# A two-layer encoder kernel on one core: operand sums of the feed-forward part in tiles of their own, split sooner, another order of units in the down projection, and one more weight group by Strassen's scheme

## The chip, the cores and the metric

The kernel runs on one core of a Trainium2 chip. The metric is the device time of one execution in microseconds (us). The time shown for a kernel is the median of its runs.

## The reference, cut to what matters

Two layers work on 512 tokens of width 1024. Each has a token mixer, cross attention into 256 memory tokens and an output projection, which this change leaves alone, and then the feed-forward part:

```
def conv_ffn(h, w_up, conv_w, conv_b, w_down):
    u = h @ w_up                       # 1024 -> 5632
    c = depthwise causal convolution of u over the tokens, width 3, + conv_b
    a, g = jnp.split(c, 2, axis=-1)    # 2816 each
    return (jax.nn.silu(g) * a) @ w_down
...
h = rms_norm(x, ffn_norm[i])
x = x + conv_ffn(h, w_up[i], conv_w[i], conv_b[i], w_down[i])
```

All of it is in fp32.

## The kernel before, in words

**Products.** An fp32 operand is split into a rounded high part and the low remainder (`parts_of`, L1277 to L1279 for activations: the cast on ScalarE at L1278, the subtraction on VectorE at L1279). A product is three matmuls, high by high, high by low and low by high (`product`, L407 to L409). Weights come by DMA into a `raw` tile and are split into `whi` and `wlo` (cast on ScalarE, subtraction on VectorE, L257 and L260).

**Strassen's scheme.** Where the text says "seven", a 2x2 block of products is formed from 7 products instead of 8, with 256 columns in the moving operand instead of 512. That needs sums of the operands. Sums of weights are made on GpSimd: `block_sums` issues four additions (L285) into a tile `wsum`, of which there are two, and `combined` splits the raw part (L308, L309) and the sums (L311, L312). `SEVEN` (L140) lists which groups of the up projection go this way: the halves "ua" 5, 6, 8 and 9 of both layers. `up_by_seven` (L1213 to L1244) forms them, with one copy on ScalarE (L1238) and six additions on VectorE (L1239 to L1244) behind the matmuls.

**The feed-forward part.** `ffn` works through 11 groups of 256 hidden columns in three parts of 4, 4 and 3 groups. For each group there is a block "ua" (the half a) and a block "ug" (the gate g) of the up projection, each with two halves n = 0, 1 of 128 columns. `conv` (L1248 on VectorE, L1250 on ScalarE, L1251 and L1252 on VectorE) follows each, then the gate's silu (L1446, ScalarE), the product with a (L1448, VectorE) into a tile `cvo`, and the split of that product into two tiles `mid`. Behind a part's last group comes the down projection of the part (`down`), in four blocks c of 256 output columns. In the last part of layer 0 all four blocks, and in the last part of layer 1 the block 3, use eight products and no sums; the others use seven. A unit (c, m) is the contribution of the part's group m to block c: seven steps of three matmuls. Three of the steps, `own`, need only the group's own `mid` tiles: steps 1 and 2 those of its half n = 0, step 0 that of n = 1. Four, `mixed`, need sums of the two halves: steps 5 and 4 the first two sums, steps 6 and 3 the other two.

**Sums of the activations.** `mid_sums` calls `combine` (L1281 to L1290), four subtractions of 128x256. For the last group of a part they run on VectorE into two `cvo` tiles, and their split follows at once. For the other groups they run on GpSimd into one `wsum` tile of 128x1024, from the same two buffers as the sums of weights, and their split is put off: `behind` places it after the third `conv` that follows (`convs[0] == 3`).

**What sets the order.** TensorE runs in the order of the program. For VectorE, ScalarE and GpSimd a list scheduler orders the instructions when the kernel is built. In `down` the units (0, 0) to (0, nq-2) and (1, 0) come first, then, to give the last group's sums time, `own` of (0, nq-1), `own` of (1, 1), `mixed` of (0, nq-1), `mixed` of (1, 1), and so on. When a block c is complete, `decode` (L1369 to L1377) adds its four PSUM banks into the residual stream. The banks are taken in rotation, so block 2 gets those of block 0.

```
own, mixed = steps[:3], steps[3:]
seq = [(0, m, steps) for m in range(nq - 1)] + [(1, 0, steps), (0, nq - 1, own), (1, 1, own), (0, nq - 1, mixed)]
seq += [(1, 1, mixed)] + [(1, m, steps) for m in range(2, nq)]
```

Of the kernel before, what the change touches and what calls it, by code (L numbers as in the profile page):

```python
# [11 lines left out]
F32 = mybir.dt.float32  # L12
# [9 lines left out]
S = 512  # L22
# [114 lines left out]
    return out  # L137


SEVEN = [("ua", l, q) for l in range(2) for q in (5, 6, 8, 9)]  # L140
SUMS_AT = {1:(4,5),2:(0,1),3:(2,3)}
TURNS = ('mm', 'mm', 'sm', 'sm', 'lg', 'lg', 'tp', 'tp')

# [41 lines left out]
def trunk(ctx, tc, head_d, x_t, mem_t, wpack, cols_a_d, cols_d, conv_d, gate_d, rel_bias, diff_lambda, consts, onehot, out):  # L185
    nc = tc.nc
    mm = nc.tensor.matmul
    V, A, G = nc.vector, nc.scalar, nc.gpsimd
# [65 lines left out]
    at = [0]  # L254
# [70 lines left out]
    def sum_tile():  # L325
        return sum_pool[0].tile([128, WTILE], F32, name="wsum", bufs=2)
# [172 lines left out]
    E = mybir.EngineType  # L499
    load = nc.sync.dma_start  # L500
    with tc.tile_pool(name="ini", bufs=1) as ip, tc.manual_schedule(engines={E.Activation, E.DVE, E.Pool, E.SP}):
# [34 lines left out]
        parts, acc, split_w = [], [None], [None]  # L536
# [631 lines left out]
    def ffn(pool, l, acc):  # L1168
# [37 lines left out]
            refill()  # L1206

        def ctile():
            return pool.tile([128, S], F32, name="cvo", bufs=6)

        def up(i, n):
            p, = take(1)
# [34 lines left out]
        def conv(p, j):  # L1247
            V.tensor_mul(p, p, rB)  # L1248
            c = ctile()
            first = A.activation(c, p, AF.Identity, scale=cv[l][:, 2, j:j + 1], bias=cv[l][:, 3, j:j + 1])  # L1250
            V.scalar_tensor_tensor(c[:, 1:], p[:, :S - 1], cv[l][:, 1, j:j + 1], c[:, 1:], op0=ALU.mult, op1=ALU.add)  # L1251
            final = V.scalar_tensor_tensor(c[:, 2:], p[:, :S - 2], cv[l][:, 0, j:j + 1], c[:, 2:], op0=ALU.mult, op1=ALU.add)  # L1252
            if later:
                convs[0] += 1
                if convs[0] == 3:
                    convs[0] = 0
                    behind(first, final)
            return c
# [19 lines left out]
            A.copy(hi, t)  # L1278
            V.tensor_sub(lo, t, hi.bitcast(F32))  # L1279

        def combine(b2, b1, bh, bl, fh, fl, E, parts):  # L1281
            t = [ctile(), ctile()] if E is V else [sum_tile()]
            q = [blk(i, 256) for i in range(4)]
            at = lambda i: t[i // 2][:, q[i % 2]] if E is V else t[0][:, q[i]]
            for i, x, y in ((0, b1[:, right], b1[:, left]), (1, b2[:, right], at(0)), (2, b2[:, right], b1[:, right]),
                            (3, b2[:, left], at(1))):
                ins = E.tensor_sub(at(i), x, y)  # L1287
                if E is G:
                    tc.keep_in_program_order(ins)
            parts(t)  # L1290
            return q
# [6 lines left out]
        def mid_sums(c2, ops, E):  # L1298
            h, lo = (pool.tile([128, 2 * S], F32R, name="mid2", bufs=8) for _ in range(2))

            def parts(t):
                for i, x in enumerate(t):
                    c = blk(i, 2 * S // len(t))
                    if E is V:
                        parts_of(x, h[:, c], lo[:, c])
                    else:
                        later.append((x, h[:, c], lo[:, c]))
            q = combine(*c2, *ops, E, parts)
            return operands([h[:, c] for c in q], [lo[:, c] for c in q], *ops)

        later, convs = [], [0]
# [8 lines left out]
        def scaled(k):  # L1320
            t = ctile()
            A.activation(t, xT[k], AF.Copy, scale=c_ffn(l, k))
            return t

        def token_sums(ks):
            (bh, bl), (fh, fl) = (tokens[k] for k in ks)
            tiles = [split_tiles(pool, "vs", 12) for _ in range(2)]

            def parts(t):
                for i, (hi, lo) in enumerate(tiles):  # L1330
                    parts_of(t[0][:, blk(i, S)], hi, lo)
            combine(scaled(ks[0]), scaled(ks[1]), None, None, None, None, G, parts)
            h, lo = ([t[i][:, c] for t in tiles for c in (left, right)] for i in range(2))
            sums_of[ks] = operands(h, lo, bh, bl, fh[:, left], fl[:, left])

        place = [(2, left), (0, left), (0, right), (1, left), (1, right), (2, right), (3, left)]
        steps, close = (1, 2, 0, 5, 4, 6, 3), {2: 0, 5: 2, 6: 3, 3: 1}

        def down(base, nq, mids, pairs, last, acc2):
            first = used[0]  # L1340
            whole = [plan[first + c][0][0] == "dw" for c in range(4)]
            banks, seen = {}, [set() for _ in range(4)]

            def start(c):
                begin(("dw" if whole[c] else "dn", l, base, c))
                banks[c] = take(2 if whole[c] else 4)

            def emitted(c, m):
                if m == nq - 1 or m % 2:
                    release(first + c, 1 if whole[c] else 2, m == nq - 1)  # L1350

            def seven(c, m, some=steps):
                while len(made) <= first + c or len(made[first + c]) <= m:
                    refill()
                for i in some:
                    b, h = place[i]
                    (hi, lo), (bh, bl) = made[first + c][m][i], mids[m][i]
                    for t, (w, v) in enumerate(((hi, bh), (hi, bl), (lo, bh))):
                        mm(banks[c][b][:, h], w, v, start=b not in seen[c], stop=m == nq - 1 and t == 2 and i in close)  # L1359
                        seen[c].add(b)  # L1360
                if some[-1] != steps[-1]:
                    return
                emitted(c, m)
                if m == nq - 1:
                    decode(c)

            def decode(c):
                b, x1, x2, u, y = banks[c], xT[2 * c], xT[2 * c + 1], ctile(), ctile()[:, left]
                A.copy(u[:, left], b[2][:, left])  # L1369
                V.tensor_add(x1, x1, b[0])  # L1370
                V.tensor_add(y, u[:, left], b[2][:, right])
                V.tensor_add(u[:, right], y, b[1][:, right])
                V.tensor_add(y, y, b[3][:, left])
                V.tensor_add(x2, x2, b[1])
                V.tensor_add(x1, x1, u)
                x2v = x2.rearrange("p (h c) -> p h c", h=2)
                V.tensor_add(x2v, x2v, y.unsqueeze(1).to_broadcast([128, 2, 256]))  # L1377
                if last and l == 1:
                    for n in (2 * c, 2 * c + 1):
                        nc.sync.dma_start(out[n], xT[n])  # L1380

            def eight(c, n, m0, m1, total=nq):
                parts = whole_piece(first + c)
                product(banks[c][n], parts, n, pairs, range(2 * m0, 2 * m1), 2 * total)

            if all(whole):
                for c0 in (0, 2):
                    cs = (c0, c0 + 1)
                    for c in cs:
                        start(c)  # L1390
                        for n in range(2):
                            eight(c, n, 0, nq - 1)
                        emitted(c, 1)
                    for c in cs:
                        for n in range(2):
                            eight(c, n, nq - 1, nq)
                            update(2 * c + n, banks[c][n], lambda k: c_attn(1, k), acc2)
                            nc.sync.dma_start(xres[2 * c + n], xT[2 * c + n])
                        emitted(c, nq - 1)
                return  # L1400
            own, mixed = steps[:3], steps[3:]
            seq = [(0, m, steps) for m in range(nq - 1)] + [(1, 0, steps), (0, nq - 1, own), (1, 1, own), (0, nq - 1, mixed)]
            seq += [(1, 1, mixed)] + [(1, m, steps) for m in range(2, nq)]
            seq += [(c, m, steps) for c in ((2,) if whole[3] else (2, 3)) for m in range(nq)]
            for c, m, some in seq:
                if c not in banks:
                    start(c)
                seven(c, m, some)
            if whole[3]:
                start(3)  # L1410
                eight(3, 0, 0, nq)
                V.tensor_add(xT[6], xT[6], banks[3][0])
                nc.sync.dma_start(out[6], xT[6])
                eight(3, 1, 0, nq - 1, nq - 1)
                V.tensor_add(xT[7], xT[7], banks[3][1])
                for t, p, queue in zip((left, right), take(2), (nc.sync, nc.scalar)):
                    p = p[:, :S // 2]
                    parts = made[first + 3]
                    product(p, parts[-2:], 1, [(bh[:, t], bl[:, t]) for bh, bl in pairs[-2:]])
                    V.tensor_add(xT[7][:, t], xT[7][:, t], p)  # L1420
                    queue.dma_start(out[7, :, t], xT[7][:, t])

        base, acc2 = 0, None
        for part, nq in enumerate(HALVES):
            mids, pairs = [], []
            last = part == len(HALVES) - 1
            for q in range(base, base + nq):
                c2, ops, at, cs = [], [], {}, {}
# [11 lines left out]
                for n in range(2):  # L1440
# [13 lines left out]
                    else:  # L1454
                        m = mid_tile()
# [104 lines left out]
```

## Time and profile before

| | |
|---|---|
| median of three runs | 1152.81 us (1152.59 to 1152.91) |
| profiled execution | 1153.93 us |
| its span | 1152.0 us |
| granted TensorE clock | 1.00 |
| TensorE busy | 1141.9 us, 99% |
| VectorE busy | 931.4 us, 81% |
| ScalarE busy | 616.4 us, 54% |
| GpSimd busy | 270.1 us, 23% |

Times in the views below count from the start of the span. In a timeline each row gives the start, the time from the start of the row's first to the end of its last instruction, the engine, line and operation, the tiles, and in brackets the idle time before it with what ended it. A matmul's own duration runs past the start of the next, since matmuls are pipelined; what counts is the distance between starts. TensorE's rows in the down projection are L1359.

### The profile page before, as it was taken

How to read it: one execution, taken by the hardware profiler on the slowest of the kernel's cores; microseconds unless marked ns; L12 is line 12 of the kernel's file. 1: busy time of each engine (PE TensorE's matmuls, PEld its weight loads, DVE VectorE, ACT ScalarE, POOL GpSimd, SP SyncE). 2: the span in 40 equal slices, each digit the busy share in tenths (PEclk: the TensorE clock that was granted, in tenths of full speed). 3: DMA queues.
4: the chain of work that ended last, by engine and by line, in shares of the span. 5: the costliest groups of instructions: out<-in, count | busy, mean ns of one | idle time of the engine just before them, and what ended most of it. 6: DMA issues, size and time to landing. Idle time of an engine off the chain costs nothing.

```text
span 1152.0 us, 17410 instructions
## 1 busy us (share of the span) xinstructions
PE 1141.9 (99%) x6527; PEld 993.4 (86%) x6527; DVE 931.4 (81%) x1531; ACT 616.4 (54%) x1080; POOL 270.1 (23%) x318
## 2 busy tenths in 40 slices
PE   9999999999999999999999999999999999999998
PEld 7888888888889888898888888988888989899888
DVE  7676778688889789999677637777898988999987
ACT  6676686556554454445457634535664434544552
POOL 0000000003364423740000000000245432476241
PEclk9999999999999999999999999999999999999999
DMA  8522242133314332344252220333232343224312
GB/s 286 175 82 87 78 142 74 57 109 92 110 56 146 93 92 73 93 128 126 71 176 73 94 97 16 92 126 126 73 92 74 95 126 104 89 76 137 105 51 101
DMA packets 39666, 117.86 MB, mean 102 GB/s; under 512 B 4768, under 2 KB 7257, under 8 KB 39583
## 3 DMA queue, kind: packets, MB, share of 16 engines
q1 hardware_dynamic: 39150, 116.37, 32.0%
q8 instruction: 51, 0.84, 0.3%
q10 hardware_dynamic: 432, 0.39, 0.1%
q14 instruction: 33, 0.26, 0.1%
HBM read 112.54 MB, written 4.21 MB: 101 GB/s over the span
## 4 chain that ended last, share of the span: by engine, by line
PE 80%; DVE 13%; ACT 4%; issue 2%; POOL 1%; ACTq 0%; POOLq 0%; DVEq 0%
PE ps_mm L385 6%; PE ps_mm L408 6%; PE ps_mm L407 6%; PE ps_mm L409 6%; PE ps_mm L387 6%; PE ps_mm L386 6%; PE ps_lg L1359 3%; PE ps_sm L408 3%; PE ps_sm L407 3%; PE ps_sm L409 3%; PE ps_mm L1359 3%; PE ps_tp L224 3%; PE ps_lg L1233 3%; PE ps_tp L1359 2%; PE ps_sm L1359 2%; DVE mid L1279 2%
## 5 line engine op out<-in xcount | busy, mean ns | idle before, releaser
L260 DVE TENSOR_TENSOR wlo<-raw,whi 128x1024 fp32r<-128x1024 f32 (+5 forms) x166 | 188.7, 1148 | 74.7 <-ACT whi L257 73.8
L257 ACT CAST whi<-raw 128x1024 fp32r<-128x1024 f32 (+5 forms) x166 | 157.9, 967 | 104.9 <-PE ps_mm L408 24.3
L385 PE MATMUL ps_mm<-whi,xsh 128*128 128x512 f32 (+2 forms) x328 | 126.3, 385 | 0.0
L387 PE MATMUL ps_mm<-whi,xsl 128*128 128x512 f32 (+2 forms) x328 | 123.0, 375 | 0.0
L386 PE MATMUL ps_mm<-wlo,xsh 128*128 128x512 f32 (+2 forms) x328 | 122.8, 374 | 0.0
L407 PE MATMUL ps_mm<-xsh,whi 128*128 128x512 f32 x310 | 121.8, 393 | 0.0
L408 PE MATMUL ps_mm<-xsl,whi 128*128 128x512 f32 x310 | 120.9, 390 | 0.0
L409 PE MATMUL ps_mm<-xsh,wlo 128*128 128x512 f32 x310 | 120.8, 390 | 0.0
L285 POOL TENSOR_TENSOR wsum<-raw 128x256 f32<-128x256 f32 (+1 forms) x108 | 87.8, 834 | 117.5 <-DMA raw<-in_wpack_dram 64.1
L1287 POOL TENSOR_TENSOR wsum<-cvo 128x256 f32<-128x256 f32 x40 | 33.9, 848 | 226.7 <-DVE cvo L1448 140.9
L407 PE MATMUL ps_sm<-xsh,whi 128*128 128x512 f32 x202 | 78.6, 389 | 0.0
L408 PE MATMUL ps_sm<-xsl,whi 128*128 128x512 f32 x202 | 78.6, 389 | 0.0
L409 PE MATMUL ps_sm<-xsh,wlo 128*128 128x512 f32 x202 | 78.6, 389 | 0.0
L312 DVE TENSOR_TENSOR wlo<-wsum,whi 128x1024 fp32r<-128x1024 f32 (+1 forms) x54 | 70.6, 1307 | 8.9 <-ACT whi L311 8.9
L311 ACT CAST whi<-wsum 128x1024 fp32r<-128x1024 f32 (+1 forms) x54 | 51.9, 962 | 39.8 <-POOL wsum L285 39.5
L385 PEld LDWEIGHTS ps_mm<-whi,xsh 128*128 128x128 f32 x328 | 61.7, 188 | 11.4 <-issue 1.0
L387 PEld LDWEIGHTS ps_mm<-whi,xsl 128*128 128x128 f32 x328 | 61.7, 188 | 11.3
L386 PEld LDWEIGHTS ps_mm<-wlo,xsh 128*128 128x128 f32 x328 | 61.8, 188 | 10.1
L409 PEld LDWEIGHTS ps_mm<-xsh,wlo 128*128 128x128 f32 x310 | 58.2, 188 | 12.1
L407 PEld LDWEIGHTS ps_mm<-xsh,whi 128*128 128x128 f32 x310 | 58.2, 188 | 11.9 <-issue 0.3
L408 PEld LDWEIGHTS ps_mm<-xsl,whi 128*128 128x128 f32 x310 | 58.3, 188 | 11.9 <-DVE xsl L366 0.4
L1263 POOL MEMSET xsh<- 128x128 f32 x2 | 0.4, 210 | 277.5 <-PE ps_sm L408 191.0
(428 smaller groups left out, 3144.9 us busy)
## 6 DMA issues: line engine op xcount, KB each, us to landing
raw<-in_wpack_dram SPq DMA_DIRECT2D x178, 512.0 KB, 3.6
xt<-in_x_t_dram SPq DMA_DIRECT2D x15, 256.0 KB, 5.2
raw<-in_wpack_dram SPq DMA_DIRECT2D x15, 256.0 KB, 2.8
raw<-in_wpack_dram SPq DMA_DIRECT2D x8, 384.0 KB, 3.3
xres<-xt SPq DMA_DIRECT2D x8, 256.0 KB, 3.4
xt<-xres SPq DMA_DIRECT2D x8, 256.0 KB, 5.7
out_dram<-xt SPq DMA_DIRECT2D x7, 256.0 KB, 2.0
bt<-bias_d SPq DMA_DIRECT2D x6, 256.0 KB, 4.3
```

The lines of the kernel that those rows point to most:

```text
L257: ins = A.copy(hi[:, c], raw[:, c])
L260: V.tensor_sub(lo[:, c], raw[:, c], hi[:, c].bitcast(F32))
L285: tc.keep_in_program_order(getattr(G, "tensor_" + op)(o, x, y))
L311: A.copy(h1[:, m], wsum[:, m])
L312: V.tensor_sub(l1[:, m], wsum[:, m], h1[:, m].bitcast(F32))
L385: mm(p, sh[k][:, blk(b)], hi, start=k == 0, stop=False)
L386: mm(p, sh[k][:, blk(b)], lo, start=False, stop=False)
L387: mm(p, sl[k][:, blk(b)], hi, start=False, stop=k == KT - 1)
L407: mm(p, hi[:, blk(n)], bh, start=i == first, stop=False)
L408: mm(p, hi[:, blk(n)], bl, start=False, stop=False)
L409: mm(p, lo[:, blk(n)], bh, start=False, stop=i == last)
L1359: mm(banks[c][b][:, h], w, v, start=b not in seen[c], stop=m == nq - 1 and t == 2 and i in close)
```

## The change

Five edits. `SEVEN` gains the gate half of group 9 in layer 0. The sums of activations that GpSimd makes go into two `cvo` tiles of their own instead of a `wsum` tile, so that their split is two of 128x512 instead of one of 128x1024; there are seven `cvo` buffers instead of six. Their split is placed after the second `conv` instead of the third. In `down`, for parts of four groups, unit (1, 1) comes whole ahead of the last group's unit (0, 3), which comes whole too; for the part of three groups the order stays. The scratch memory for descriptors of dynamic DMAs is halved.

```
-SEVEN = [("ua", l, q) for l in range(2) for q in (5, 6, 8, 9)]
+SEVEN = [("ua", l, q) for l in range(2) for q in (5, 6, 8, 9)] + [("ug", 0, 9)]
...
-            return pool.tile([128, S], F32, name="cvo", bufs=6)
+            return pool.tile([128, S], F32, name="cvo", bufs=7)
...
-                if convs[0] == 3:
+                if convs[0] == (2):
...
-        def combine(b2, b1, bh, bl, fh, fl, E, parts):
-            t = [ctile(), ctile()] if E is V else [sum_tile()]
+        def combine(b2, b1, E, t, parts):
...
-            q = combine(*c2, *ops, E, parts)
+            q = combine(*c2, E, [ctile(), ctile()], parts)
...
-            combine(scaled(ks[0]), scaled(ks[1]), None, None, None, None, G, parts)
+            combine(scaled(ks[0]), scaled(ks[1]), G, [sum_tile()], parts)
...
-            seq = [(0, m, steps) for m in range(nq - 1)] + [(1, 0, steps), (0, nq - 1, own), (1, 1, own), (0, nq - 1, mixed)]
-            seq += [(1, 1, mixed)] + [(1, m, steps) for m in range(2, nq)]
+            seq = [(0, m, steps) for m in range(nq - 1)] + [(1, 0, steps)]
+            if nq > 3:
+                seq += [(1, 1, steps), (0, nq - 1, steps)] + [(1, m, steps) for m in range(2, nq)]
+            else:
+                seq += [(0, nq - 1, own), (1, 1, own), (0, nq - 1, mixed), (1, 1, mixed), (1, 2, steps)]
...
-    nc = _bacc.Bacc("TRN2", target_bir_lowering=False, num_devices=1, dynamic_dma_scratch_size=512)
+    nc = _bacc.Bacc("TRN2", target_bir_lowering=False, num_devices=1, dynamic_dma_scratch_size=256)
```

Three places show how instructions move; the numbers in names are those of the buffers. The first is TensorE behind unit (1, 0) in the first part of layer 0, in the kernel before: `mid_3313` and `mid_3411` belong to the last group, `mid_2943` to group 1.

```order
L1359 MATMUL ps_mm_3426<-mid_3313,whi_3342 128x256
...
L1359 MATMUL ps_mm_3426<-mid_3313,whi_3344 128x256
...
L1359 MATMUL ps_sm_3428<-mid_3411,whi_3342 128x256 x2
...
L1359 MATMUL ps_lg_3508<-mid_2943,whi_3382 128x256
...
L1359 MATMUL ps_lg_3508<-mid_2943,whi_3384 128x256
...
L1359 MATMUL ps_tp_3510<-mid_3040,whi_3382 128x256 x2
...
L1359 MATMUL ps_sm_3428<-mid2_3414,whi_3344 128x256
```

And in the changed kernel, where `mid_2948` and `mid_3043` belong to group 1 and `mid_3324` and `mid_3420` to the last group.

```order
L1358 MATMUL ps_lg_3517<-mid_2948,whi_3393 128x256
...
L1358 MATMUL ps_tp_3519<-mid_3043,whi_3393 128x256 x2
...
L1358 MATMUL ps_tp_3519<-mid2_3063,whi_3395 128x256
...
L1358 MATMUL ps_lg_3518<-mid2_3063,whi_3393 128x256
...
L1358 MATMUL ps_mm_3435<-mid_3324,whi_3353 128x256
...
L1358 MATMUL ps_sm_3437<-mid_3420,whi_3353 128x256 x2
```

Where the last group's first step stood, group 1's unit (1, 1) now stands, with all its seven steps; the last group's first step, its step 0 and its first mixed step come behind it. The first and the step 0 are issued 21 matmuls later than before, the mixed ones 12, since 9 matmuls of (1, 1) stood ahead of those already.

The second place is VectorE at the end of the same part, from the last group's two halves on, in the kernel before (L1448 is the product with the gate, `mid2` the split of sums, L309 and L312 the splits of weights).

```order
L1448 TENSOR_TENSOR cvo_3302<-cvo_3302,cvo_3307 128x512
...
L1279 TENSOR_TENSOR mid2_3230<-wsum_3231,mid2_3229 128x1024
L1248 TENSOR_TENSOR ps_tp_3357<-ps_tp_3357,rB_2659 128x512
L312 TENSOR_TENSOR wlo_3385<-wsum_3352,whi_3384 128x1024
...
L1448 TENSOR_TENSOR cvo_3398<-cvo_3398,cvo_3405 128x512
...
L1279 TENSOR_TENSOR mid_3411<-cvo_3398,mid_3411 128x256
...
L1279 TENSOR_TENSOR mid2_3415<-cvo_3416,mid2_3414 128x512
L312 TENSOR_TENSOR wlo_3475<-wsum_3392,whi_3474 128x1024
L1279 TENSOR_TENSOR mid2_3415<-cvo_3417,mid2_3414 128x512
```

The same in the changed kernel (there L1450 is the product).

```order
L1279 TENSOR_TENSOR mid2_3236<-cvo_3237,mid2_3235 128x512
L1279 TENSOR_TENSOR mid2_3236<-cvo_3238,mid2_3235 128x512
L1450 TENSOR_TENSOR cvo_3309<-cvo_3309,cvo_3314 128x512
...
L1248 TENSOR_TENSOR ps_tp_3368<-ps_tp_3368,rB_2659 128x512
L312 TENSOR_TENSOR wlo_3396<-wsum_3363,whi_3395 128x1024
...
L1450 TENSOR_TENSOR cvo_3409<-cvo_3409,cvo_3414 128x512
...
L1279 TENSOR_TENSOR mid_3420<-cvo_3409,mid_3420 128x256
...
L1279 TENSOR_TENSOR mid2_3424<-cvo_3425,mid2_3423 128x512
L1279 TENSOR_TENSOR mid2_3424<-cvo_3426,mid2_3423 128x512
L312 TENSOR_TENSOR wlo_3484<-wsum_3403,whi_3483 128x1024
```

The split of the earlier group's sums has left the stretch between the last two products, and the split of weights that stood between the last two splits of sums stands behind both.

The third place is VectorE a little further on, at the decode of block 0, in the kernel before.

```order
L1370 TENSOR_TENSOR xt_1738<-xt_1738,ps_mm_3426 128x512
L1371 TENSOR_TENSOR cvo_3579<-cvo_3578,ps_sm_3428 128x256
L1372 TENSOR_TENSOR cvo_3578<-cvo_3579,ps_mm_3427 128x256
L309 TENSOR_TENSOR wlo_3564<-raw_3350,whi_3563 128x2x384
L1373 TENSOR_TENSOR cvo_3579<-cvo_3579,ps_sm_3429 128x256
L312 TENSOR_TENSOR wlo_3566<-wsum_3482,whi_3565 128x1024
L1374 TENSOR_TENSOR xt_1740<-xt_1740,ps_mm_3427 128x512
```

And in the changed kernel, where the decode's lines are lower by one.

```order
L309 TENSOR_TENSOR wlo_3564<-raw_3361,whi_3563 128x2x384
L1369 TENSOR_TENSOR xt_1738<-xt_1738,ps_mm_3435 128x512
L312 TENSOR_TENSOR wlo_3566<-wsum_3491,whi_3565 128x1024
L309 TENSOR_TENSOR wlo_3600<-raw_3401,whi_3599 128x2x384
L312 TENSOR_TENSOR wlo_3602<-wsum_3573,whi_3601 128x1024
L1370 TENSOR_TENSOR cvo_3615<-cvo_3614,ps_sm_3437 128x256
L1371 TENSOR_TENSOR cvo_3614<-cvo_3615,ps_mm_3436 128x256
L1373 TENSOR_TENSOR xt_1740<-xt_1740,ps_mm_3436 128x512
L1372 TENSOR_TENSOR cvo_3615<-cvo_3615,ps_sm_3438 128x256
```

All but the first addition of the decode stand behind four splits of weights, the last of which needs a sum of weights (`wsum_3573`) that GpSimd can start only when the L312 behind the last two splits of sums (that of `wsum_3403` in the place before) has freed its buffer.

More of the change, by code (lines that the diff above doesn't have):

```diff
@@ L1279, in parts_of @@
             V.tensor_sub(lo, t, hi.bitcast(F32))
-        def combine(b2, b1, bh, bl, fh, fl, E, parts):
-            t = [ctile(), ctile()] if E is V else [sum_tile()]
+        def combine(b2, b1, E, t, parts):
             q = [blk(i, 256) for i in range(4)]
-            at = lambda i: t[i // 2][:, q[i % 2]] if E is V else t[0][:, q[i]]
+            at = lambda i: t[i // 2][:, q[i % 2]] if len(t) > 1 else t[0][:, q[i]]
             for i, x, y in ((0, b1[:, right], b1[:, left]), (1, b2[:, right], at(0)), (2, b2[:, right], b1[:, right]),
```

## Prediction

> **What bounds the kernel now.** I read the page's first part, then the chain that ended last, then the waits of TensorE. From the page, first part and the chain by engine:
>
> ```profile
> span 1152.0 us, 17410 instructions
> PE 1141.9 (99%) x6527; PEld 993.4 (86%) x6527; DVE 931.4 (81%) x1531; ACT 616.4 (54%) x1080; POOL 270.1 (23%) x318
> PE 80%; DVE 13%; ACT 4%; issue 2%; POOL 1%; ACTq 0%; POOLq 0%; DVEq 0%
> ```
>
> TensorE is busy 99% of the span, so only two things can shorten the kernel: fewer matmul cycles, or less of the little time in which TensorE waits. The chain nevertheless runs 13% over VectorE, which says that VectorE's results come just in time somewhere. The waits of TensorE say where:
>
> ```profile
> PE ps_tp L1359 <- DVE mid L1279: 3.2, 4, 1.3
> PE ps_sm L1359 <- DVE mid L1279: 2.7, 4, 0.8
> ```
>
> Eight waits, all of the down projection (L1359) for a split of activations (L1279). The worst place is the second part of layer 0; TensorE's timeline there:
>
> ```profile
> 466.38 0.40 PE L1359 MATMUL ps_lg<-mid,whi 128*128 128x256 f32 x2
> ...
> 467.10 0.31 PE L1359 MATMUL ps_tp<-mid,whi 128*128 128x256 f32 x1
> 468.67 0.39 PE L1359 MATMUL ps_tp<-mid,whi 128*128 128x256 f32 x1 [1.27 <-DVE mid L1279]
> ...
> 470.81 0.39 PE L1359 MATMUL ps_tp<-mid,whi 128*128 128x256 f32 x1 [0.44 <-DVE mid L1279]
> ...
> 472.55 0.38 PE L1359 MATMUL ps_tp<-mid,whi 128*128 128x256 f32 x1 [0.76 <-DVE mid L1279]
> ...
> 474.68 0.40 PE L1359 MATMUL ps_mm<-mid,whi 128*128 128x256 f32 x2
> ```
>
> At 466.38 the `own` steps of unit (0, 3) begin, at 474.68 unit (1, 2). Between them stand two units, 42 matmuls. The chain gives the distance of two such matmuls when nothing waits:
>
> ```profile
> 345.00 1.08 PE ps_lg L1359 x9
> ```
>
> 1.08/9 = 0.120 us, so two units need 5.04 us. They took 8.30: 3.26 us lost at three stops, at step 0 (467.10), at the first mixed step (470.81) and at the third (472.55). The same stretch in the first part of layer 0 and in the three parts of layer 1, each by its first row and the row that follows it:
>
> ```profile
> 338.75 0.40 PE L1359 MATMUL ps_mm<-mid,whi 128*128 128x256 f32 x2
> ...
> 345.20 0.40 PE L1359 MATMUL ps_lg<-mid,whi 128*128 128x256 f32 x2
> ...
> 892.87 0.40 PE L1359 MATMUL ps_mm<-mid,whi 128*128 128x256 f32 x2
> ...
> 900.63 0.40 PE L1359 MATMUL ps_lg<-mid,whi 128*128 128x256 f32 x2
> ...
> 1021.81 0.40 PE L1359 MATMUL ps_lg<-mid,whi 128*128 128x256 f32 x2
> ...
> 1028.01 0.40 PE L1359 MATMUL ps_mm<-mid,whi 128*128 128x256 f32 x2
> ...
> 1124.91 0.40 PE L1359 MATMUL ps_lg<-mid,whi 128*128 128x256 f32 x2
> ...
> 1130.33 0.40 PE L1359 MATMUL ps_mm<-mid,whi 128*128 128x256 f32 x2
> ```
>
> They lose 6.45 - 5.04 = 1.41, 7.76 - 5.04 = 2.72, 6.20 - 5.04 = 1.16 and, for the part of three groups, 5.42 - 5.04 = 0.38. With 3.26 that is **8.93 us**, all that the waits can give. It is more than the 5.9 of the waits view, since a wait inside a group of two rows isn't listed there and the first matmul behind a stop runs longer.
>
> **The change part by part.**
>
> *The order of units.* With unit (1, 1) whole in front, step 0 of the last group is asked for 21 matmuls later, 2.52 us, and its mixed steps 12 matmuls later, 1.44 us (9 of (1, 1) stood ahead of these already). With VectorE's times as they are, the first and fourth part of four groups lose nothing any more (1.41 and 1.16 are below 1.44). The second, with 3.26, keeps 1.82: the first stop goes, its mixed steps come 1.44 later. The third, with 2.72, keeps 1.28. Gain 1.41 + 1.44 + 1.44 + 1.16 = 5.45 us. Nothing else is queued behind these matmuls than matmuls; the DMA queues keep their order.
>
> *The split of weights between the two splits of sums.* VectorE's timeline in the second part of layer 0:
>
> ```profile
> 458.32 1.75 DVE L1279 TENSOR_TENSOR mid<-wsum,mid 128x1024 fp32r<-128x1024 f32 x1
> ...
> 461.79 1.37 DVE L312 TENSOR_TENSOR wlo<-wsum,whi 128x1024 fp32r<-128x1024 f32 x1 [1.10 <-ACT whi L311]
> ...
> 470.07 0.68 DVE L1279 TENSOR_TENSOR mid<-cvo,mid 128x512 fp32r<-128x512 f32 x1
> 470.68 1.22 DVE L312 TENSOR_TENSOR wlo<-wsum,whi 128x1024 fp32r<-128x1024 f32 x1
> 471.81 0.68 DVE L1279 TENSOR_TENSOR mid<-cvo,mid 128x512 fp32r<-128x512 f32 x1
> ```
>
> In the new order L312 stands behind both splits, so the second split starts 471.81 - 470.68 = 1.13 us sooner. Of the 1.82 left in this part, the first mixed step is still late by about 0.8: it is asked for at 466.38 + 30 x 0.120 = 469.98, and its split ends at 470.75. The third mixed step no longer adds anything. In the third part some 0.15 stays. Further gain 1.02 + 1.13 = 2.15 us.
>
> *Tiles of their own, split sooner.* The chain to the last product runs through VectorE in order. Out of it, between the last two convs, goes the split of 1024 at 458.32, some 1.68 us; into it, ahead of the first half's product, come two splits of 512, at the 0.6 from one start to the next that 470.07 and 470.68 show: 1.2. And the wait of 1.10 ahead of L312 at 461.79 goes. It has its source on GpSimd:
>
> ```profile
> 456.14 1.44 POOL L285 TENSOR_TENSOR wsum<-raw 128x256 f32<-128x256 f32 x2 [3.49 <-DVE wlo L312]
> 457.55 1.45 POOL L285 TENSOR_TENSOR wsum<-wsum,raw 128x256 f32<-128x256 f32 x1
> ```
>
> The sum of weights waited 3.49 us for one of two `wsum` buffers, the other being held by the sum of activations until its split at 458.32. Now weights alone use both. So the last product comes about 0.48 + 1.10 = 1.6 us sooner. The 0.8 and 0.15 above are within that: gain 0.95 us, which makes 8.55 for the parts of four groups. For the part of three groups, where no such wait for L311 stands, I take 0.3 of its 0.38 (ends: 0 and 0.38). The seventh `cvo` buffer and the smaller scratch issue nothing; with two more `cvo` tiles held from sum to split the bound is a wait of a conv's L1250 for a tile, which I take as 0, since the split that frees them is placed sooner.
>
> A rule weighs against this step. The Trainium skill, SBUF — State Buffer, section "SBUF: two separate sides", has VectorE with two SBUF inputs and GpSimd lock a shared port pair for a whole instruction, the other being blocked. The trace fits roughly: the split at 458.32 overlaps GpSimd's 457.55 to 459.00 and takes 1.75 where 470.68 shows 1.22 for the same size, 0.53 of the 0.68 that a full block would add. By the rule each of the two earlier splits could lose up to 0.7 us beside GpSimd, and the 1.6 would become 0.2 (rival 1); without it 1.6 stands.
>
> *Group 9's gate by seven.* TensorE's timeline has a "ua" block by seven and behind it a "ug" block by eight; VectorE's has their costs; the windows view sums layer 0's last part and what follows, 493.30 to 590.10:
>
> ```profile
> 499.88 0.40 PE L407 MATMUL ps_lg<-xsh,whi 128*128 128x512 f32 x1
> ...
> 510.18 0.40 PE L407 MATMUL ps_mm<-xsh,whi 128*128 128x512 f32 x1
> ...
> 521.09 0.39 PE L407 MATMUL ps_sm<-xsh,whi 128*128 128x512 f32 x1
> ```
> ```profile
> 509.71 0.42 DVE L1239 TENSOR_TENSOR cvo<-cvo,ps_tp 128x256 f32<-128x256 f32 x1 [1.34 <-ACT cvo L1238]
> ...
> 513.83 0.69 DVE L1244 TENSOR_TENSOR ps_lg<-ps_lg,cvo 128x512 f32<-128x512 f32 x1
> ...
> 519.74 1.22 DVE L260 TENSOR_TENSOR wlo<-raw,whi 128x1024 fp32r<-128x1024 f32 x1
> ```
> ```profile
> sum 96.80, PE 96.80 PEld 83.84 DVE 78.04 ACT 45.32 POOL 11.11; mean PE 24.20 PEld 20.96 DVE 19.51 ACT 11.33 POOL 2.78
> ```
>
> By seven 10.30 us, by eight 10.91: **0.61 us** less. VectorE gets six additions, 4 x 0.42 + 2 x 0.69 = 3.1 us at most, and splits 3200 columns of weights instead of 2048, 1152/1024 x 1.22 = 1.4 us: 4.5 us. GpSimd gets eight more additions. VectorE has 96.80 - 78.04 = 18.8 us free there, which hides it; without that cover it costs 4.5 us.
>
> *A new queue at the decode.* In the new order four splits of weights stand ahead of the decode's L1370 (L1371 before), and the last needs a sum that GpSimd starts only when the L312 behind the splits of sums has freed `wsum`. From the second part of layer 0, GpSimd, ScalarE, VectorE:
>
> ```profile
> 472.02 1.76 POOL L285 TENSOR_TENSOR wsum<-raw 128x256 f32<-128x256 f32 x2 [4.03 <-ACT cvo L1369]
> ...
> 474.56 1.34 POOL L285 TENSOR_TENSOR wsum<-raw,wsum 128x256 f32<-128x256 f32 x1
> 477.07 1.89 POOL L285 TENSOR_TENSOR wsum<-raw 128x256 f32<-128x256 f32 x2 [1.16 <-DVE wlo L312]
> ...
> 480.19 1.34 POOL L285 TENSOR_TENSOR wsum<-raw,wsum 128x256 f32<-128x256 f32 x1
> ```
> ```profile
> 473.71 1.05 ACT L311 CAST whi<-wsum 128x1024 fp32r<-128x1024 f32 x1
> ```
> ```profile
> 475.55 1.44 DVE L312 TENSOR_TENSOR wlo<-wsum,whi 128x1024 fp32r<-128x1024 f32 x1
> ```
>
> Call T0 the start of unit (1, 1), 466.38. L312, which ended at 471.90, comes one split (0.6) later and 1.6 to 2.6 sooner (2.6 if the splits sooner fall into idle time): T0 + 3.5 to 4.5. The sum takes 472.02 to 475.90 = 3.9, the cast 1.05, the split 1.44, L1370 0.42: T0 + 10.3 to 11.3. Unit (2, 0), four units behind T0, needs the bank that L1370 frees at its seventh matmul, T0 + 10.08 + 0.72 = **10.80**, and L1373's and L1372's about as tightly. So between 0.5 to spare and 0.5 to 0.8 short; I take a wait of 0.3 in this part. The third has 0.5 more room, the first and fourth 1.8 and 2.1 (their stretches lost 1.85 and 2.10 less), so 0 there.
>
> **Sum.** 8.55 + 0.3 + 0.61 - 0.3 = 9.16 us. The profiled execution took 1153.93 (span 1152.0 and 1.93 around it), 1.12 above the median; the terms are differences and hold for both: 1153.93 - 9.16 = 1144.77, and from the median 1152.81 - 9.16 = **1143.6 us**.
>
> **Rivals.**
>
> 1. *The last product doesn't come sooner.* If the earlier splits cost the chain what they spare, as by the rule above, 0.95 and the 0.3 fail, though the decode's wait may grow: 7.6 + 0.61 = 8.2, 1144.6. If VectorE's order gives nothing at all, the order of units alone is left: 5.45 + 0.61 = 6.1, 1146.7. For it: VectorE has hardly any idle time between 458 and 466. Against: the 1.10 and 3.49 of wait have one cause, which goes. Chance 0.20.
> 2. *The decode's queue bites in several parts.* With 4.5 us for GpSimd's sum (477.07 to 481.53, its slower one) and 1.75 for the split (458.32) the chain is 0.9 longer: some 1.2 to 1.7 in the second, 0.7 to 1.2 in the third part, 0 in the others, so 2 to 3 us in place of 0.3: 1145.3 to 1146.3. Chance 0.14.
> 3. *The same queue, slower than before.* If GpSimd's sum starts only when (1, 1) and (0, 3) are over (a late `raw` tile or a late L312), at T0 + 5.04, with 4.5, 1.05, a further split of 1.44 ahead, 1.44 and 0.42, L1370 ends at T0 + 13.9: 3.1 us in each of four parts, 12.4, more than the 9.46 of gain: 1152.81 + 2.9 = 1155.8. It decides against the change once L1370 ends behind T0 + 10.80 + 9.46/4 = 13.2 in all four. The chain above stands 1.9 us or more off that. Chance 0.04.
> 4. *Group 9's cost isn't hidden,* or the stalls stay as they are because another wait holds the last product: in the first case 4.5 us and eight blocks of 0.7 on VectorE, 10 us, against 9.2: 1153.7 less what idle time takes; in the second 1152.81 - 0.61 = 1152.2. Chance 0.05 for no change.
>
> **How the numbers follow.** Forecast, 1143.0 to 1144.4: 0.57. Rival 1: 0.20, rival 2: 0.14, rival 3: 0.04, rival 4: 0.05. The range runs from the whole 8.93 + 0.61 with a little room, 1142.8, to the end of rival 1, 1147.0. A measurement of this kernel can tell about 0.2%, 2.3 us, from no change. Faster by more: 0.57 + 0.20 + 0.14 = 0.91; within: 0.05; slower: 0.04.
>
> **What would show it.** The waits of TensorE should have no L1279 of any weight any more, at most 0.1 in the part of three groups, and the two units at T0 should take 5.04 us in all four parts. The split of sums should be two of 128x512 ahead of the first half's product, L312 without a wait for L311 there, and the last product 1.6 us sooner against T0. Group 9's two blocks should take 10.3 us each. A wait of TensorE (L1358 in the changed kernel) for L1370 to L1373 at unit (2, 0) would be rival 2 or 3; waits for L1279 in the second part of layer 0 rival 1; a wait at the conv of group 10 rival 4.

## The result: a third of the forecast gain

The changed kernel took 1149.66 us (13 runs, 1149.17 to 1150.36), the kernel before 1152.99 us beside it (13 runs). The ratio is 0.9972, with a 95% interval of 0.9965 to 0.9979: 3.3 us faster, where 9.16 had been forecast and 1143.6 us named. The range ended at 1147.0.

The page of the changed kernel's profile (execution 1149.61, span 1147.8), first part and chain by engine:

```profile
span 1147.8 us, 17525 instructions
PE 1139.8 (99%) x6554; PEld 993.0 (87%) x6554; DVE 932.1 (81%) x1553; ACT 618.8 (54%) x1097; POOL 279.3 (24%) x326
PE 95%; POOL 2%; DVE 1%; ACT 1%; issue 1%; DMA 0%; SPq 0%; POOLq 0%; ACTq 0%
```

VectorE's share of the chain fell from 13% to 1%, and GpSimd's rose from 1% to 2%. TensorE's waits in the changed kernel:

```profile
PE ps_tp L1358 <- DVE cvo L1370: 1.7, 2, 0.8
PE ps_sm L1358 <- DVE cvo L1370: 1.6, 2, 1.2
PE ps_tp L512 <- PEq L1517: 0.8, 1, 0.8
```

No row names L1279 any more: all 8.93 us of stalls for splits went, in all five parts. In their place stand waits for L1370, an addition of the decode, four in all. TensorE's timeline at unit (2, 0) of the second part of layer 0:

```profile
475.84 0.40 PE L1358 MATMUL ps_lg<-mid,whi 128*128 128x256 f32 x2
...
476.20 0.40 PE L1358 MATMUL ps_lg<-mid,whi 128*128 128x256 f32 x2
...
477.56 0.48 PE L1358 MATMUL ps_tp<-mid,whi 128*128 128x256 f32 x2 [0.84 <-DVE cvo L1370]
...
478.61 0.47 PE L1358 MATMUL ps_lg<-mid,whi 128*128 128x256 f32 x2
```

The seventh matmul of the unit, due at 475.84 + 6 x 0.12 = 476.56, starts at 477.56; after it the next bank is late by a further 0.27. Counted as the distance of starts above the undisturbed 0.12, this stop costs 1.41 us, and those of the other three parts of four groups 0.93, 1.78 and 1.41: 5.5 us in all. So 8.93 + 0.61 - 5.5 = 4.0 us should be left as a gain, and the spans of the two profiles differ by 4.2.

VectorE's timeline there shows the queue that the change put ahead of L1370:

```profile
467.80 1.21 DVE L312 TENSOR_TENSOR wlo<-wsum,whi 128x1024 fp32r<-128x1024 f32 x1
468.94 0.94 DVE L309 TENSOR_TENSOR wlo<-raw,whi 128x768 fp32r<-128x768 f32 x1
469.81 0.67 DVE L1369 TENSOR_TENSOR xt<-xt,ps_lg 128x512 f32<-128x512 f32 x1
470.40 1.21 DVE L312 TENSOR_TENSOR wlo<-wsum,whi 128x1024 fp32r<-128x1024 f32 x1
471.54 0.94 DVE L309 TENSOR_TENSOR wlo<-raw,whi 128x768 fp32r<-128x768 f32 x1
475.71 1.37 DVE L312 TENSOR_TENSOR wlo<-wsum,whi 128x1024 fp32r<-128x1024 f32 x1 [3.23 <-ACT whi L311]
477.00 0.41 DVE L1370 TENSOR_TENSOR cvo<-cvo,ps_tp 128x256 f32<-128x256 f32 x1
```

VectorE idles 3.23 us at the last L312, with L1370, whose operands are there (the second experiment shows it), behind it. What L312 waits for comes from ScalarE's L311, and that from GpSimd's sum:

```profile
469.15 3.93 POOL L285 TENSOR_TENSOR wsum<-raw 128x256 f32<-128x256 f32 x2 [4.96 <-ACT whi L308]
473.05 0.73 POOL L285 TENSOR_TENSOR wsum<-wsum,raw 128x256 f32<-128x256 f32 x1
473.86 0.74 POOL L285 TENSOR_TENSOR wsum<-raw,wsum 128x256 f32<-128x256 f32 x1
474.55 1.45 POOL L285 TENSOR_TENSOR wsum<-raw 128x256 f32<-128x256 f32 x2
```

GpSimd's row names L308 as what ended its wait, but it starts 0.14 us after the L312 at 467.80 has ended (469.01), and by the program's order it is that L312 whose buffer it takes. The sum lasts from 469.15 to 474.60, 5.45 us. Its first two additions take 3.93, the same pair at 474.55, with VectorE idle until 475.71, 1.45. In the first part of layer 0, whose stop is the smallest, the same sum begins at 341.70 and lasts until 347.00:

```profile
341.70 2.16 POOL L285 TENSOR_TENSOR wsum<-raw 128x256 f32<-128x256 f32 x2 [4.97 <-issue]
343.81 1.76 POOL L285 TENSOR_TENSOR wsum<-wsum,raw 128x256 f32<-128x256 f32 x1
345.66 1.34 POOL L285 TENSOR_TENSOR wsum<-raw,wsum 128x256 f32<-128x256 f32 x1
```

The last product, which the prediction wanted 1.6 us sooner against T0 (the start of unit (1, 1), or of what stood in its place before), comes sooner by 2.2 us in this part. In the kernel before it starts 1.02 us ahead of T0 = 466.38, in the changed kernel 3.21 us ahead of T0 = 465.76:

```profile
465.36 1.16 DVE L1448 TENSOR_TENSOR cvo<-cvo 128x512 f32<-128x512 f32 x1 [0.76 <-ACT cvo L1446]
```
```profile
462.55 1.04 DVE L1450 TENSOR_TENSOR cvo<-cvo 128x512 f32<-128x512 f32 x1 [0.76 <-ACT cvo L1448]
```

Group 9's two blocks took 10.27 and 10.30 us, as forecast.

### The profile page after: what moved, and what is told of

Its sections match the earlier page's. It is cut to its first block, busy times and chain, and to the rows that moved or that the text cites. A ratio compares the mean times of both kernels' runs of the same rounds, so it can differ in the third digit from the quotient of the medians.

```text
span 1147.8 us, 17525 instructions
## 1 busy us (share of the span) xinstructions
PE 1139.8 (99%) x6554; PEld 993.0 (87%) x6554; DVE 932.1 (81%) x1553; ACT 618.8 (54%) x1097; POOL 279.3 (24%) x326
## 4 chain that ended last, share of the span: by engine, by line
PE 95%; POOL 2%; DVE 1%; ACT 1%; issue 1%; DMA 0%; SPq 0%; POOLq 0%; ACTq 0%
PE ps_mm L407 6%; PE ps_mm L408 6%; PE ps_mm L409 6%; PE ps_mm L385 6%; PE ps_mm L387 6%; PE ps_mm L386 6%; PE ps_sm L408 4%; PE ps_sm L409 4%; PE ps_sm L407 4%; PE ps_lg L1358 4%; PE ps_mm L1358 3%; PE ps_tp L1358 3%; PE ps_tp L224 3%; PE ps_lg L1233 3%; PE ps_tp L408 3%; PE ps_tp L407 3%
## 5 line engine op out<-in xcount | busy, mean ns | idle before, releaser
L260 DVE TENSOR_TENSOR wlo<-raw,whi 128x1024 fp32r<-128x1024 f32 (+5 forms) x165 | 185.8, 1137 | 75.3 <-ACT whi L257 73.6
L285 POOL TENSOR_TENSOR wsum<-raw 128x256 f32<-128x256 f32 (+1 forms) x112 | 99.5, 909 | 119.9 <-DMA raw<-in_wpack_dram 71.6
L407 PE MATMUL ps_mm<-xsh,whi 128*128 128x512 f32 x294 | 115.5, 393 | 0.0
L408 PE MATMUL ps_mm<-xsl,whi 128*128 128x512 f32 x294 | 114.6, 390 | 0.0
L409 PE MATMUL ps_mm<-xsh,wlo 128*128 128x512 f32 x294 | 114.5, 389 | 0.0
L312 DVE TENSOR_TENSOR wlo<-wsum,whi 128x1024 fp32r<-128x1024 f32 (+1 forms) x56 | 69.0, 1232 | 15.2 <-ACT whi L311 15.0
L1286 POOL TENSOR_TENSOR cvo<-cvo 128x256 f32<-128x256 f32 x56 | 47.4, 865 | 134.5 <-DVE cvo L1450 133.4
L311 ACT CAST whi<-wsum 128x1024 fp32r<-128x1024 f32 (+1 forms) x56 | 53.5, 956 | 36.5 <-POOL wsum L285 29.5
L409 PEld LDWEIGHTS ps_mm<-xsh,wlo 128*128 128x128 f32 x294 | 55.2, 188 | 11.6
L407 PEld LDWEIGHTS ps_mm<-xsh,whi 128*128 128x128 f32 x294 | 55.2, 188 | 11.3 <-issue 0.3
L408 PEld LDWEIGHTS ps_mm<-xsl,whi 128*128 128x128 f32 x294 | 55.3, 188 | 11.2 <-DVE xsl L366 0.4
```

Of the source, the lines that this page charges most:

```text
L260: V.tensor_sub(lo[:, c], raw[:, c], hi[:, c].bitcast(F32))
L285: tc.keep_in_program_order(getattr(G, "tensor_" + op)(o, x, y))
L311: A.copy(h1[:, m], wsum[:, m])
L312: V.tensor_sub(l1[:, m], wsum[:, m], h1[:, m].bitcast(F32))
L407: mm(p, hi[:, blk(n)], bh, start=i == first, stop=False)
L408: mm(p, hi[:, blk(n)], bl, start=False, stop=False)
```

## The experiments

The theory after this: the new order of units makes the kernel slower, since it releases the weights of block 1 sooner, and so the splits of block 2's weights are issued ahead of the decode of block 0; the gain comes from the other edits. The rival: the tiles and the earlier splits crowd VectorE and GpSimd, and the decode would be late in any order.

**The changed kernel with the old order of units.**

```
-            seq = [(0, m, steps) for m in range(nq - 1)] + [(1, 0, steps)]
-            if nq > 3:
-                seq += [(1, 1, steps), (0, nq - 1, steps)] + [(1, m, steps) for m in range(2, nq)]
-            else:
-                seq += [(0, nq - 1, own), (1, 1, own), (0, nq - 1, mixed), (1, 1, mixed), (1, 2, steps)]
+            seq = [(0, m, steps) for m in range(nq - 1)] + [(1, 0, steps), (0, nq - 1, own), (1, 1, own), (0, nq - 1, mixed)]
+            seq += [(1, 1, mixed)] + [(1, m, steps) for m in range(2, nq)]
```

> The changed kernel with the old order of units in the down projection; tiles of their own, the earlier split and group 9 stay. Theory (the new order of units puts four splits of weights ahead of the decode of block 0, and the wait of TensorE for L1370 at unit (2, 0), 0.8 to 1.6 us in each of four parts, comes from that order alone): no wait for L1370, no wait for L1279 either or 0.4 us at most, since the last splits of sums now end before the old order asks for them; 4.5 to 5 us faster than the changed kernel, 1144.5 to 1145.3 us. Rival (the decode's wait comes from the tiles and the earlier splits, which crowd VectorE and GpSimd): the waits for L1370 stay and the stalls for L1279 come back in part, 1149 to 1152 us.

1144.29 us, ratio 0.9931 (0.9918 to 0.9943). That is 5.4 us below the changed kernel's median, and 5.0 if each is taken against the kernel before as it ran beside it (8.35 and 3.3 us faster). TensorE's waits have one row left, at the kernel's start:

```profile
PE ps_tp L512 <- PEq L1514: 0.8, 1, 0.8
```

Neither L1370 nor L1279 is waited for. The theory holds; the new order of units cost 5.0 to 5.4 us, the 5.5 us of stops, and was not needed for the stalls.

**The decode written ahead of the release, with the new order of units.**

```
-                emitted(c, m)
                 if m == nq - 1:
                     decode(c)
+                emitted(c, m)
```

> The changed kernel with the decode of a block written ahead of the release of its weights, so that VectorE's L1370 stands ahead of the last split of weights that needs GpSimd's sum; the new order of units stays. Theory (the queue on VectorE is the cause): no wait of TensorE for L1370 to L1373, 4.5 to 5 us faster than the changed kernel, 1144.5 to 1145.3 us. Rival (TensorE waits for the bank because of the copy on ScalarE, or GpSimd's sum itself is late for unit (2, 2)): a wait of about 1 us in each part stays under another name, 1148 to 1150 us.

1144.66 us, ratio 0.9934 (0.9921 to 0.9946). VectorE's timeline at the same place, with L1370 ahead of the last two splits:

```profile
469.39 1.21 DVE L312 TENSOR_TENSOR wlo<-wsum,whi 128x1024 fp32r<-128x1024 f32 x1
470.53 0.41 DVE L1370 TENSOR_TENSOR cvo<-cvo,ps_tp 128x256 f32<-128x256 f32 x1
470.86 1.17 DVE L309 TENSOR_TENSOR wlo<-raw,whi 128x768 fp32r<-128x768 f32 x1
...
475.07 1.76 DVE L312 TENSOR_TENSOR wlo<-wsum,whi 128x1024 fp32r<-128x1024 f32 x1
```

GpSimd's sum is no sooner, and the last L312 starts at 475.07, 10.3 us after T0 (464.75 here) against 9.95 in the changed kernel; but nothing that TensorE is about to need stands behind it. L1370 could run at 470.53. So the queue on VectorE is the cause: a late copy on ScalarE or a late sum on GpSimd would have held TensorE here too.

**The new order of units alone,** in the kernel before (the `seq` lines of the change, no other edit).

> The kernel before with the new order of units alone. Theory: the stalls for L1279 shrink by 5.4 us, as the prediction had it, but the four splits of weights stand ahead of the decode here too, and L312 of the second split is later than in the changed kernel, so that TensorE waits some 1.2 us for L1370 in each of four parts, 4.8 in all: 0.3 to 1.5 us faster than before, 1151.5 to 1152.7 us. Rival (the decode's wait needs the tiles and earlier splits): 5.4 us faster, 1147.5 us.

1158.93 us, ratio 1.0055 (1.0042 to 1.0068): slower than before by 6.3 us, and 6 us above what was expected. The waits of TensorE:

```profile
PE ps_sm L1359 <- DVE cvo L1371: 3.7, 2, 1.9
PE ps_tp L1359 <- DVE cvo L1371: 3.5, 2, 1.9
```

The decode (L1371 here) makes TensorE stop for 2.0, 2.0, 2.0 and 1.76 us instead of 1.2. And behind two of these stops TensorE ran slower. The windows view gives the window and its length, the busy time of TensorE, then of the weight loads, VectorE, ScalarE and GpSimd, and the granted clock as the third number from the end:

```profile
352.00:357.00 5.00, 4.89 (x29) 4.72 (x28) 5.00 (x7) 1.05 (x1) 4.92 (x5) 0.66 0.00 0
357.00:362.00 5.00, 5.00 (x45) 5.00 (x44) 4.96 (x9) 1.79 (x2) 0.03 (x1) 1.00 0.35 105
483.00:487.00 4.00, 4.00 (x22) 4.00 (x23) 4.00 (x6) 1.04 (x1) 3.89 (x5) 0.57 0.00 0
```

The 0.66 and 0.57 are means of windows that are in part at full clock: in windows of 1 us within them (354 to 356, 484 to 486) the granted clock is 0.50. It lasts 3.4 us each time, and some 17 matmuls stand 0.213 us apart instead of 0.12: 1.6 us lost each time.

**The order of units alone, with the decode first** (both edits above, in the kernel before).

> The kernel before with the new order of units, and with the decode of a block written ahead of the release of its weights (no tiles, no group 9). It tests the prediction's first step by itself. Theory (the order of units is worth 5.4 us of stalls for L1279 once nothing stands ahead of the decode; the slow run of the units alone, 1158.9, was the wait for L1371 of 2 us in each of four parts and the low granted clock that followed it): no wait for L1371, no stretch of lower clock, stalls of 1.8, 1.3 and 0.4 us left, 1147 to 1148 us. Rival (the order of units costs in another way too): 1150 us or more.

1148.47 us, ratio 0.9965 (0.9953 to 0.9978): 4.3 us faster than before, 2.5 to 5.4 by the interval, against 5.4 forecast for this step. No wait for the decode is left and no slow stretch. TensorE's waits:

```profile
PE ps_tp L1359 <- DVE mid L1279: 0.9, 2, 0.8
...
PE ps_sm L1359 <- DVE mid L1279: 0.8, 1, 0.8
PE ps_lg L1359 <- DVE wlo L312: 0.5, 1, 0.5
```

As reckoned, stalls stay in the second part of layer 0 (1.0), in the first of layer 1 (1.3) and in the part of three groups (0.5); the prediction had 1.82, 1.28 and 0.38. A new one of 0.9 for L312 in that last part had not been foreseen. Together they are 3.7 us, so by the distances of starts 5.2 of the 8.93 us are gone, nearly what was forecast.

**The other edits alone: tiles of their own, seven buffers and the earlier split,** with the smaller scratch, old units, no group 9.

> The kernel before with the tiles of their own, seven cvo buffers, the earlier split and the smaller scratch, but with the old units and without group 9. Theory: the whole 8.9 us of stalls goes, 1144 to 1145 us, 0.6 us above the changed kernel with the old units. Rival (the stalls need the new order of units): 2 to 4 us faster than before, 1149 to 1151 us.

1144.88 us, ratio 0.9934 (0.9921 to 0.9948). All stalls are gone without the new order of units. Against 1144.29 with group 9's gate, that gate is worth 0.59 us; 0.61 had been forecast.

**Which of these edits does it?** The split put back behind the third conv, own tiles kept (with old units and group 9):

```
-                if convs[0] == (2):
+                if convs[0] == 3:
```

> The changed kernel with the old units, and with the split of GpSimd's sums again after the third conv; tiles of their own and group 9 stay. Theory (the place of the split matters most, since there it stands between the last two convs, and L312 stands between the last two splits again): the stalls come back in the second part of layer 0 and the first of layer 1, 1.5 to 2 and 0.5 to 1.2 us: 1146 to 1147.5 us. Rival (it is the freed wsum buffers that matter): within 0.5 us of the 1144.3 with the split after the second conv.

1153.82 us, ratio 1.0008 (1.0000 to 1.0017). The whole gain is gone: it is 9.5 us slower than with the split after the second conv, where I expected 2 to 3. The waits of TensorE, and VectorE in the second part of layer 0:

```profile
PE ps_tp L1358 <- DVE mid L1279: 2.7, 4, 1.1
PE ps_tp L1358 <- ACT mid L1278: 1.9, 2, 0.9
PE ps_sm L1358 <- DVE mid L1279: 1.4, 4, 0.6
```
```profile
456.70 1.36 DVE L312 TENSOR_TENSOR wlo<-wsum,whi 128x1024 fp32r<-128x1024 f32 x1 [1.10 <-ACT whi L311]
457.99 1.23 DVE L1279 TENSOR_TENSOR mid<-cvo,mid 128x512 fp32r<-128x512 f32 x1
...
461.96 2.37 DVE L1279 TENSOR_TENSOR mid<-cvo,mid 128x512 fp32r<-128x512 f32 x2
```

Both things that the prediction's third step was to remove are there: a wait of 1.10 for L311, and the split between the last two convs. The wait stands one L312 earlier than in the kernel before, and GpSimd has no wait for a `wsum` buffer ahead of that sum (its additions follow each other from 451.60), so the held buffer was not the only source of such a wait. The split's two pieces now take 2.37 us, where the one split took 1.75; they run beside a GpSimd sum (459.77 to 463.77).

**One `wsum` tile again, the split after the second conv** (old units and group 9):

```
-            q = combine(*c2, E, [ctile(), ctile()], parts)
+            q = combine(*c2, E, [ctile(), ctile()] if E is V else [sum_tile()], parts)
```

> The changed kernel with the old units, and with GpSimd's sums of activations again in one wsum tile of the two; the split after the second conv and group 9 stay. Theory (the place of the split matters most): few stalls, 0 to 1 us, 1144.3 to 1145.5 us. Rival (the freed wsum buffers matter most): GpSimd's sums of weights wait for a buffer as before, ScalarE's L311 and VectorE's L312 behind it, and 2 us or more of stalls stay, 1146.5 us or more.

1143.86 us, ratio 0.9925 (0.9912 to 0.9939), no stalls. With the early split, the tiles of their own bring nothing that can be measured.

**One digit alone.** The kernel before with `convs[0] == 2`, nothing else, and the same with group 9's gate:

> The kernel before with one digit changed: the split of GpSimd's sums after the second conv instead of the third (one wsum tile, six cvo buffers, old units, no group 9). Theory (the place of the split is all that the gain rests on, since the last product and its splits then come early enough for the old units): no stalls for L1279, 1144 to 1145 us. Rival (with six cvo buffers a conv waits for a tile, or the tiles of their own are needed after all): 1 us or more of stalls, 1146 us or more.

> The same with the gate half of group 9 of layer 0 by seven. By the difference of the runs with and without it so far (1144.29 and 1144.88) 0.6 us less than the split alone; 1143.5 to 1144.3 us.

1144.68 us (0.9932, 0.9918 to 0.9945) and 1144.10 us (0.9925, 0.9912 to 0.9937). VectorE in the second part of layer 0 with the one digit:

```profile
447.16 1.60 DVE L1279 TENSOR_TENSOR mid<-wsum,mid 128x1024 fp32r<-128x1024 f32 x1
448.69 1.22 DVE L1448 TENSOR_TENSOR cvo<-cvo 128x512 f32<-128x512 f32 x1
...
456.91 1.21 DVE L312 TENSOR_TENSOR wlo<-wsum,whi 128x1024 fp32r<-128x1024 f32 x1
...
460.32 1.16 DVE L1448 TENSOR_TENSOR cvo<-cvo 128x512 f32<-128x512 f32 x1 [0.76 <-ACT cvo L1446]
...
465.04 1.28 DVE L1279 TENSOR_TENSOR mid<-cvo,mid 128x512 fp32r<-128x512 f32 x2
```

The split stands ahead of the first half's product. L312 at 456.91 doesn't wait; the two last splits follow each other, with L312 behind them. One moved instruction does what three edits were credited with; with the own tiles, the seventh buffer and the smaller scratch beside it the time was 1144.88. Which part of its effect counts most, the `wsum` buffer that comes free sooner or the place between the last two convs that is left empty, was not separated.

**Group 9's gate by seven in layer 1 too** (with old units): `[("ug", l, 9) for l in range(2)]`.

> The changed kernel with the old units, and with the gate half of group 9 by seven in layer 1 too. By counting of matmuls 0.6 us less, 1143.7 us, if VectorE and GpSimd have room in layer 1's last part; a wait for the decode or for L1279 in layer 1's last part if they have not, up to 3 us.

1150.77 us, ratio 0.9984 (0.9976 to 0.9993), 6.5 us slower than with layer 0's alone. The waits of TensorE, all in the last part of layer 1:

```profile
PE ps_lg L1358 <- DVE cvo L1252: 2.7, 2, 1.6
PE ps_mm L1358 <- DVE mid L1279: 1.0, 1, 1.0
...
PE ps_mm L1358 <- ACT mid L1278: 0.6, 1, 0.6
```

The last convs come late: four stops of 1.89, 1.20, 0.74 and 1.29 us, 5.1 us in all as distances of starts, and a slow stretch of 1.6 us behind the fourth. The first and the fourth:

```profile
1115.26 0.47 PE L1358 MATMUL ps_lg<-mid,whi 128*128 128x256 f32 x2 [1.62 <-DVE cvo L1252]
...
1121.26 0.38 PE L1358 MATMUL ps_mm<-mid,whi 128*128 128x256 f32 x1 [1.02 <-DVE mid L1279]
```

The granted clock stays at 1.00 behind the first and falls to 0.50 at 1122.0. A likely reason for the late convs is that three of the four blocks of the down projection in this part are by seven and need VectorE and GpSimd too, while none is in layer 0's last part; no run tested it.

## Why the prediction was wrong, by its steps

- **What can be won** was right in kind: 8.93 us of stalls for L1279 and 0.61 for group 9. All stalls went, the part of three groups included, where only 0.3 of 0.38 had been counted. The gate measured 0.59.
- **The step that failed is the new queue at the decode.** Its mechanism was right: L1370 behind a split that needs a sum whose buffer L312 frees. Its size was taken as 0.3 us in one part; it was 0.93, 1.41, 1.78 and 1.41, 5.5 us in all, and undoing it gave 5.0 to 5.4. Two links were mis-sized. GpSimd's sum was put at 3.9 us, from a place where VectorE alternates such splits with additions from PSUM, and at 4.5 in rival 2. It took 5.45 beside VectorE's splits from SBUF (5.30, 5.45, 5.44 and 5.16 in the four parts). And the first, third and fourth parts were given 1.8, 0.5 and 2.1 us more room than the second, because they had lost less before. Measured from T0 (338.64, 465.76, 889.73 and 1017.70), that sum starts at T0 + 3.06, 3.39, 3.77 and 3.68. Start and length of the sum together differ from part to part just as the four stops do. The room that the prediction gave those parts was not there, because the earlier split moved the last product by a different amount in each part: it started 2.9, 1.0, 1.6 and 3.1 us ahead of T0 before the change and 3.6, 3.2, 2.8 and 3.2 after it, so the parts that had been late gained most and all four ended up nearly alike. A smaller stall before doesn't mean that the chain behind the change comes that much sooner. Rival 2 was this mechanism, with too small a price (2 to 3 us) and with 0 for the first and fourth parts.
- **The order of units** was worth 4.3 us by itself once the decode was out of its way, against 5.4 (5.2 by the stalls in the trace); but with the decode as the code has it, it was a loss of 6.3 us alone and of 5.0 to 5.4 in the change. In the sum it was the first and largest term, and it wasn't needed: the stalls go without it.
- **Tiles of their own** were credited with freeing the `wsum` buffers. With own tiles and the late split nothing is won; with the early split and one `wsum` tile as much is won as with both. The step gave the right sum for the wrong edit.
- **The rule of the shared port** would have taken the 1.6 us to 0.2 and put the time at 1144.6. The two earlier splits do take 2.04 us in the changed kernel (at 449.32) where two of 512 took 1.28 elsewhere (at 466.60), but all stalls went all the same. Its effect is seen on GpSimd instead, in the sum of 5.45 us: the Trainium skill, SBUF — State Buffer, "SBUF: two separate sides", would have each of VectorE's three splits from 468.94 to 472.48 hold GpSimd for its whole length, and the pair of additions ends 0.6 us after the last of them. The rows agree with it. The traces of all twelve kernels go further: an addition of this kind was slow only where VectorE ran an operation with two operands from SBUF beside it (the numbers are in the last section). That such operations slow the sum is borne out by this; that they do it by a lock held for the whole instruction is argued, not shown, since no run took the splits away from beside this sum.
- **The median.** The profiled execution of before was taken as 1.1 us above the median throughout. The traces of the changed kernel and of that with the old units are 4.2 and 9.8 us shorter in span than before's, their medians 3.3 and 8.35. So about 1 us of what before's profile shows was not in its median, and the terms, read from that profile, include it. In which of them it lies stays open.

## What to carry to other kernels

Where code that is moved releases a buffer sooner, look for what is then issued sooner, and on which in-order engine it lands ahead of something that was on time. Price a chain at the durations that it has beside its new neighbours. And of a bundle of edits, ask which single one already gives the result: here it was one digit, with 1144.68 us where the best versions reached 1143.9 to 1144.3.

## What the runs showed of the hardware

**The clock.** Three times in these traces the granted clock of TensorE fell to 0.50 for 3.4 us, at a cost of 1.6 us each: twice with the new order of units alone, behind stops of 2.03 us, and once with both gates by seven, from 1122.0 on, behind the stops of 0.74 and 1.29 us. In the 3.41 us before each fall TensorE was idle for 1.89, 1.87 and 1.60 us. The length of a stop doesn't decide it: behind stops of 2.00 and 1.76 us in the first of these runs and of 1.89 us in the second the clock stayed at 1.00. The two falls in one run lie 129.7 us apart, 38 times the 3.41 us that each lasted. If the clock is decided in steps of that length, the stop of 2.00 us lies across two steps, with 0.62 us of idle time in one and 1.33 in the other. That fits, but one run alone gives such a pair, and the stop of 1.76 us, with 1.60 idle in one step and no fall, shows that the limit isn't sharp at this resolution. The Trainium skill, TensorE: Matmul & The Clock Gate, Part 1, has the clock fall after an idle window of about 3.4 us; here about half of that as idle time was enough, though not always.

**GpSimd beside VectorE.** One addition of 128x256 on GpSimd (L285) took 0.72 to 0.77 us, and two in a row 1.40 to 1.46, in all 374 rows of the twelve traces during which VectorE ran no two-operand instruction (TENSOR_TENSOR) with both operands in SBUF. In 151 of these rows VectorE was adding from PSUM for 0.3 us or more. Of the 1198 rows that overlap such an instruction, 809 took over 0.1 us longer, up to 3.1 us longer for two. Whoever prices a GpSimd sum should therefore look at what VectorE runs beside it.
